# Gate and up as seven block products for eight, four token parts for three, and a down projection of its own

## The chip, the cores and the metric

The kernel runs on one core of one Trainium2 chip. Its time is the device time of one execution in microseconds; the figure of a kernel is the median of its runs. Three runs of the kernel before gave 2277.26, 2278.34 and 2279.22 us. A profile is one further execution, recorded instruction by instruction.

## The reference, cut to what matters

One decoder layer for a prompt of 1024 tokens and 8 single-token samples, so 1032 token columns. A wide input projection feeds a gated delta rule (8 heads) and a sliding-window attention; both are projected back, gated and mixed. What the change is about follows that:

```
h  = rmsnorm(x, norm1_w) * (1 + sc1) + sh1
z  = h @ w_in                       # q|k|v, gates, beta, decay, attention, two branch gates
...
mix = (sigmoid(ga) * y_a + sigmoid(gb) * y_b) @ w_o
x   = x + gt1 * mix
h2  = rmsnorm(x, norm2_w) * (1 + sc2) + sh2
gate, up = h2 @ w_ffn_gate, h2 @ w_ffn_up            # 1024 -> 2816 each
gc  = causal_dwconv(gate_ext, ffn_conv_w, L) + ffn_conv_b    # three taps along the tokens
x   = x + gt2 * ((silu(gc) * up) @ w_ffn_down)       # 2816 -> 1024
y   = rmsnorm(x, final_norm_w)
```

D_MODEL is 1024 (8 blocks of 128), D_FF is 2816 (22 tiles of 128). Beside y, the states (delta matrices, conv rows, caches, the last gate rows) are outputs. All is float32.

## The kernel before, in words

Activations lie transposed: features on the 128 partitions, tokens along the free dimension. The 1032 tokens are cut in three parts (`PARTS`, 384, 384 and 264), because a matmul's result must fit one PSUM bank. Each float32 operand is split in two float32r numbers, hi and lo (`split`, L115: a copy on ScalarE, L117, and a subtraction on VectorE, L118), and every product is three matmuls (`mm3`, L157 to L161: hi x hi, hi x lo, lo x hi). A full tile of 128 output features is 8 blocks of k, three parts and three matmuls (`project_steps`, L140): 72 matmuls, with an evacuation function called after each part. Weights come by `load_w` (L128): one DMA on SyncE's queue, then the split.

The stages, in order:
- Start and attention (0 to about 425 us): modulation vectors, the first norm (`modulate_part`, L279, which splits h part by part into the pool b1), key, query and value tiles, softmax.
- Delta rule (to about 1165): for each head `delta_prepare`, `unit_inverse` and `delta_scan` (L828, eight chunks one after the other; L843, L846, L850 and L854 are its matmuls), with the projections for head h + 2 beside them. The streams are given to `weave` (L1121) with start priorities; a planner orders the instructions of all engines by a simulated timeline and these priorities, and that order is fixed in the program. The tiles of the two branch gates (`gates`, L1144) are a generator that yields after each k: `pieces` (L746) draws 8 steps at a time, three times a head at a priority of 10000 behind the rest (L1463), and 24 times more in the last head (L743). They run in the one bank of `pmf`, ScalarE takes the tanh from it (L1157), GpSimd scales it, and a DMA stores it.
- Branches (to about 1380): what `gates` has left runs first in a plain loop (L1172), then the attention's output projection with the samples' delta rule between (`sample_delta`), then the delta rule's output projection.
- Residual and second norm (to about 1530): `residual` loads and transposes x, adds the gated w_o tiles to it (`add_gated`, L1248) and sums squares; it does so for parts 0 and 1, then for part 2, and `second_norm` (L1261) makes h2 in b1 for each part after its sums.
- Feed-forward (to about 2266): `ffn_tile` (L1342) does one gate tile and one up tile. ScalarE copies the gate out of PSUM into z (L1353), VectorE runs the three taps and the silu (L1357 to L1368), then multiplies by the up tile (L1377), and the result is split. Every two tiles, `ffn_down` (L1383) multiplies the pair before by its 128-row blocks of w_down and adds the product to x1 in SBUF, so down lies between gate and up tiles all along.
- The last norm (`last_norm`, L1400) runs part by part in the last down group.

The engine queues are in order, so an instruction that waits holds up what is behind it on its engine.

Of the kernel before, what the change touches and what calls it, by code (L numbers as in the profile page):

```python
# [28 lines left out]
PARTS = [(0, 384), (384, 384), (768, 264)]  # L29
# [28 lines left out]
class Step:  # L58
    def __init__(self, ctx, tc, I, O):
        self.ctx, self.tc, self.nc, self.I, self.O = ctx, tc, tc.nc, I, O  # L60
        self.cp = self.pool("cp", 1)
        self.dr = self.pool("dr", 1, DRAM)
        self.b1 = self.pool("b1", 1)
        self.wctx = ExitStack()
        self.where = self.pool("wp", 1, ctx=self.wctx), 2, 1
        self.pmm = self.pool("pmm", 2, PSUM)
        self.pmf = self.pool("pmf", 1, PSUM)
        self.mm, self.turn = [self.pmm], 0
        self.n, self.bufs = 0, {}
        self.lo_engine = None  # L70
        self.filler, self.ahead = iter(()), False

    def pool(self, name, bufs, space=None, ctx=None):
        kw = {} if space is None else {"space": space}
        if space != DRAM:
            kw["reuse_waits"] = "tile"
        return (ctx or self.ctx).enter_context(self.tc.tile_pool(name=name, bufs=bufs, **kw))
# [7 lines left out]
    def const(self, shape, name, dt=F32):  # L85
        return self.cp.tile(shape, dt, tag=name, name=name)
# [33 lines left out]
    def load_split(self, pool, shape, src, tag, bufs, raws, rtag="raw"):  # L120

        raw = self.t(pool, shape, rtag, bufs=raws)
# [5 lines left out]
    def load_w(self, src, width=P, where=None):  # L128

        pool, bufs, raws = where or self.where  # L130
        return self.load_split(pool, [P, KC, width], src.rearrange("(k p) c -> p k c", p=P), "w", bufs, raws)
# [8 lines left out]
    def project_steps(self, w, X, evac, parts=(0, 1, 2), psum=None):  # L140
# [16 lines left out]
    def mm3(self, ps, whi, wlo, xhi, xlo, first, last):  # L157
        mm = self.nc.tensor.matmul
        mm(ps, whi, xhi, start=first, stop=False)  # L159
        mm(ps, whi, xlo, start=False, stop=False)  # L160
        mm(ps, wlo, xhi, start=False, stop=last)  # L161

    def new_parts(self):
        return [(self.t(self.b1, [P, KC, n], f"b1h{t}", F32R), self.t(self.b1, [P, KC, n], f"b1l{t}", F32R))
# [7 lines left out]
    def vectors(self, pool, psum):  # L172
# [24 lines left out]
        nc.vector.tensor_copy(self.fcw, ps[:, 256:344].rearrange("p (j n) -> p j n", j=4))  # L197
# [72 lines left out]
    def norm_part(self, pool, t, tags):  # L270

        lo, n = PARTS[t]
# [6 lines left out]
    def modulate_part(self, pool, psum, t, xs, a, sh):  # L279

        nc = self.nc
        hi, lo = self.h[t]
        n = PARTS[t][1]
        np_ = n // P * P
        shift = self.mT[:, sh:sh + 8, :]
        if n % P:
# [6 lines left out]
            self.split(hi[:, :, np_:n], lo[:, :, np_:n], v)  # L293
        for k in range(KC):
# [8 lines left out]
            self.split(hi[:, k, :np_], lo[:, k, :np_], v)  # L303
# [93 lines left out]
    def attention(self, pool, psum):  # L397
# [19 lines left out]
        for t in range(3):  # L417
# [51 lines left out]
    def key_pair(self, pool, i, kx):  # L469
# [5 lines left out]
        def k_out(t, ps):  # L475
# [10 lines left out]
            if t == 2:  # L486
                nc.vector.tensor_copy(kx[:, i, :], ps[:, P:P + 136])  # L487
# [8 lines left out]
    def query_pair(self, pool, qt):  # L496
# [4 lines left out]
        def q_out(t, ps):  # L501
# [8 lines left out]
            if t == 2:  # L510
                nc.vector.tensor_scalar_mul(self.qs[:, qt, :], ps[:, 256:264], 0.125)
# [491 lines left out]
    def sample_delta(self):  # L1003
# [3 lines left out]
        a, b, c, d, e = (self.t(self.b1, [P, KC, PARTS[t][1]], f"b1{x}{t}", F32R).bitcast(F32).rearrange("p k n -> p (k n)")  # L1007
                         for x, t in (("h", 1), ("l", 1), ("h", 2), ("l", 2), ("h", 0)))
        small = carver(d, e)
        S0 = []  # L1010
        for h in range(H):
            S0.append((a, b, c)[h // 3][:, h % 3 * NP:h % 3 * NP + NP].rearrange("p (b v) -> p b v", b=NS))
# [68 lines left out]
        for h in range(H):  # L1081
            if h % 4 == 0:
                yield
            db = self.t(self.b1, [P, KC, 384], "b1l0", F32R).bitcast(F32).rearrange("p k n -> p (k n)") if h == 0 else db
            d = db[:, h % 3 * NP:h % 3 * NP + NP].rearrange("p (b v) -> p b v", b=NS)
# [58 lines left out]
    def gates(self):  # L1144
# [6 lines left out]
        for i, (col, dst) in enumerate(tiles):  # L1151
            w, ahead = ahead or load(i), None

            def out(t, ps):
                lo, n = PARTS[t]
                s = self.t(self.gt[0], [P, 384], self.gt[1], bufs={"gt": 2, "sgx": 3}.get(self.gt[1]))[:, :n]
# [4 lines left out]
            for t in range(3):  # L1161
                for step in self.project_steps(w, self.h, out, (t,), self.pmf):
# [4 lines left out]
    def branches(self, pool, pool2):  # L1167
        nc, I = self.nc, self.I
        ub = [self.t(pool, [P, KC, n], f"t{t}", bufs=1) for t, (_, n) in enumerate(PARTS)]
        ob = [self.load_part(pool2, self.ob, t) for t in range(3)]  # L1170
        self.fill_where, self.gt, self.ahead = self.where, (pool, "sgx"), True
# [24 lines left out]
        for t in range(3):  # L1196
# [5 lines left out]
        for t in range(3):  # L1202
# [5 lines left out]
    def gate_part(self, pool, src, t):  # L1208
        s = self.t(pool, [P, 384], "sgx", bufs=3)[:, :PARTS[t][1]]
# [4 lines left out]
    def residual(self, xpool, pool, psum):  # L1214
        nc, I = self.nc, self.I
        self.x1 = [self.t(xpool, [P, KC, n], f"x1_{t}", bufs=1) for t, (_, n) in enumerate(PARTS)]
        for t, (lo, n) in enumerate(PARTS):
            for c in range(0, n, P):
                w = min(P, n - c)
                x = self.t(pool, [P, NT], "flo", bufs=3)  # L1220
                src = I["x_prompt"][0][lo + c:lo + c + P, :] if w == P else I["x_sample"].rearrange("b s d -> (b s) d")
                nc.sync.dma_start(x[:w, :NP], src)
                for k0 in (0, 4):
                    ps = self.t(psum, [P, 4, P], "xt", bufs=2)
                    for k in range(4):
                        self.transpose(ps[:, k, :w], x[:w, (k0 + k) * P:(k0 + k + 1) * P])
                    nc.scalar.copy(self.x1[t][:, k0:k0 + 4, c:c + w], ps[:, :, :w])
        self.h2 = {}
        for parts in ((0, 1), (2,)):
            sums, last = {}, {}  # L1230

            def add(t, ps):
                self.add_gated(t, ps, j, 16)
                sq = self.t(pool, [P, 384], "nsq", bufs=2)[:, :PARTS[t][1]] if j else                     self.t(pool, [P, 384], "nss", bufs=2)[:, :PARTS[t][1]]
                nc.scalar.activation(sq, self.x1[t][:, j, :], AF.Square)
                if j == 0:
                    sums[t] = sq
                elif j < 7:
                    nc.gpsimd.tensor_tensor(sums[t], sums[t], sq, op=ALU.add)
                else:  # L1240
                    last[t] = sq

            for j in range(8):
                self.project(self.load_w(I["w_o"][0][:, j * P:(j + 1) * P]), self.mix, add, parts=parts)
            for t in parts:
                self.h2[t] = self.second_norm(pool, psum, (sums[t], last[t]), t)

    def add_gated(self, t, ps, j, m):  # L1248

        nc = self.nc  # L1250
        n = PARTS[t][1]
        np_ = n // P * P
        x = self.x1[t][:, j, :]
        nc.vector.scalar_tensor_tensor(x[:, :np_], ps[:, :np_], self.mT[:, m + j, 8:9], x[:, :np_],  # L1254
                                       op0=ALU.mult, op1=ALU.add)
        if n % P:
# [4 lines left out]
    def second_norm(self, pool, psum, squares, t):  # L1261

        nc = self.nc
        x1, a2, sh = self.x1[t], self.a2, self.mT[:, 24:32, :]
        n = PARTS[t][1]
        np_ = n // P * P
        nc_ = (n + P - 1) // P
        rs = self.t(pool, [P, 4], "rs", bufs=2)
        nc.vector.memset(rs, 1.0)
        ss = self.t(psum, [P, 4], "ss", bufs=2)  # L1270
        r = self.t(psum, [P, 512], "ss", bufs=2)
        for c in range(nc_):
            w = min(P, n - c * P)
            for i, sq in enumerate(squares):
# [246 lines left out]
```

## Time and profile before

| | us |
|---|---|
| median of 3 runs | 2278.34 |
| profiled execution | 2281.89 |
| its span, first to last instruction | 2279.8 |
| PE busy | 2175.5 (95%) |
| VectorE busy | 1258.7 (55%) |
| ScalarE busy | 732.2 (32%) |
| GpSimd busy | 221.2 (10%) |
| DMA, mean over the span | 84 GB/s |
| mean granted TensorE clock | 0.965 |

PE is TensorE's matmuls, PEld its weight loads, DVE VectorE, ACT ScalarE, POOL GpSimd, SP SyncE, which issues most DMAs. A busy time is an average over stages with different limits. A row of the groups reads: line, engine, operation, output<-inputs, shape, count | busy us, mean ns of one | idle time of the engine just before, and what ended it. Matmuls overlap in the pipeline, so the mean duration of one is not the time that one more would add; for that the distance of their starts is read from the order of time. A row of a table by stretches gives the stretch, its length, the busy time and count of each engine, the granted clock, the share of the DMA engines and GB/s.

### The profile page before, as it was taken

The numbers are of one execution on the slowest core, as the hardware profiler recorded it, in microseconds if no ns is written. First come the engines' busy times: TensorE is split into PE (matmuls) and PEld (weight loads), VectorE is DVE, ScalarE is ACT, GpSimd is POOL, SyncE is SP. The second block draws the span as 40 slices with busy tenths as digits, with TensorE's granted clock in tenths as the row PEclk, the third lists the DMA queues.
The fourth block names the chain that finished last, engine by engine and source line by source line (L and its number), as shares of the span: only waits on it lengthen the run. The fifth ranks groups of instructions, "written<-read, shape, count | busy, mean of one in ns | idle before, by whom it ended". The sixth has DMA issues, their size and how long they took to land.

```text
span 2279.8 us, 37918 instructions
## 1 busy us (share of the span) xinstructions
PE 2175.5 (95%) x15311; PEld 2043.4 (90%) x15311; DVE 1258.7 (55%) x2714; ACT 732.2 (32%) x1838; POOL 221.2 (10%) x331
## 2 busy tenths in 40 slices
PE   7998999898999999999879999999999999999998
PEld 3795888698999999999768998989999999999997
DVE  4556666665366465474232752374555555555657
ACT  3445444433333434423320223352111222111112
POOL 2000000122212112112101100210000000000000
PEclk8999998899999999999979999989999999999999
DMA  9312322322222222222432834222101111111111
GB/s 335 130 39 82 114 78 94 102 63 70 75 61 80 66 60 75 67 64 72 128 123 87 271 93 138 85 66 65 46 29 47 56 56 47 47 33 42 56 49 75
DMA packets 272768, 191.96 MB, mean 84 GB/s; under 512 B 54286, under 2 KB 248881, under 8 KB 272578
## 3 DMA queue, kind: packets, MB, share of 16 engines
q1 hardware_dynamic: 272594, 189.55, 27.4%
q8 instruction: 120, 1.97, 0.4%
q14 instruction: 54, 0.44, 0.1%
HBM read 159.62 MB, written 32.27 MB: 84 GB/s over the span
## 4 chain that ended last, share of the span: by engine, by line
PE 86%; DVE 4%; DMA 4%; ACT 2%; issue 1%; SPq 1%; POOL 0%; DVEq 0%; POOLq 0%; ACTq 0%
PE mm L159 24%; PE mm L161 24%; PE mm L160 24%; PE pv L591 1%; PE pv L589 1%; DMA qst<-in_w_mod_dram 1%; PE mm L243 1%; PE pt L169 1%; PE tp L169 1%; PE rc L850 1%; PE rc L846 1%; PE sc L552 1%; PE mm L1052 1%; PE tp L809 1%; PE tp L808 1%
## 5 line engine op out<-in xcount | busy, mean ns | idle before, releaser
L159 PE MATMUL mm<-b1h,wh 128*128 128x384 f32 (+1 forms) x2688 | 877.5, 327 | 13.7 <-DVE kx L487 4.5
L161 PE MATMUL mm<-b1h,wl 128*128 128x384 f32 (+1 forms) x2688 | 869.9, 324 | 4.0 <-DVE wl L118 4.0
L160 PE MATMUL mm<-b1l,wh 128*128 128x384 f32 (+1 forms) x2688 | 869.9, 324 | 0.3 <-DVE b1l L118 0.2
L159 PEld LDWEIGHTS mm<-b1h,wh 128*128 128x128 f32 x2688 | 511.0, 190 | 28.2 <-issue 6.3
L160 PEld LDWEIGHTS mm<-b1l,wh 128*128 128x128 f32 x2688 | 511.1, 190 | 9.6 <-issue 6.4
L161 PEld LDWEIGHTS mm<-b1h,wl 128*128 128x128 f32 x2688 | 510.4, 190 | 7.1 <-DVE wl L118 4.9
L118 DVE TENSOR_TENSOR wl<-raw,wh 128x1024 fp32r<-128x1024 f32 x136 | 166.4, 1224 | 244.6 <-ACT wh L117 243.4
L117 ACT ACTIVATE wh<-raw 128x1024 fp32r<-128x1024 f32 x137 | 144.3, 1053 | 280.1 <-PE mm L160 252.2
L1254 DVE SCALAR_TENSOR_TENSOR x<-mm,mT,x 128x384 f32<-128x384 f32 (+1 forms) x288 | 163.4, 572 | 112.2 <-PE mm L161 103.5
L159 PE MATMUL mm<-fhi,wdh 128*128 128x384 f32 (+1 forms) x528 | 170.8, 324 | 1.0 <-ACT wdh L117 0.7
L161 PE MATMUL mm<-fhi,wdl 128*128 128x384 f32 (+1 forms) x528 | 168.2, 320 | 0.3 <-DVE wdl L118 0.3
L160 PE MATMUL mm<-flo,wdh 128*128 128x384 f32 (+1 forms) x528 | 168.3, 319 | 0.0
L159 PE MATMUL mm<-b2h,wh 128*128 128x384 f32 (+1 forms) x384 | 124.4, 325 | 6.6 <-ACT b2h L117 6.6
L161 PE MATMUL mm<-b2h,wl 128*128 128x384 f32 (+1 forms) x384 | 123.4, 322 | 1.0 <-DVE wl L118 1.0
L160 PE MATMUL mm<-b2l,wh 128*128 128x384 f32 (+1 forms) x384 | 124.0, 323 | 0.3 <-DVE b2l L118 0.3
L117 ACT ACTIVATE fhi<-fa 128x384 fp32r<-128x384 f32 (+1 forms) x66 | 29.5, 485 | 223.9 <-PE mm L161 192.3
L159 PEld LDWEIGHTS mm<-fhi,wdh 128*128 128x128 f32 x528 | 99.1, 188 | 2.4 <-ACT wdh L117 1.2
L161 PEld LDWEIGHTS mm<-fhi,wdl 128*128 128x128 f32 x528 | 98.9, 188 | 1.0 <-DVE wdl L118 1.0
L160 PEld LDWEIGHTS mm<-flo,wdh 128*128 128x128 f32 x528 | 99.2, 188 | 0.0
L159 PEld LDWEIGHTS mm<-b2h,wh 128*128 128x128 f32 x384 | 73.6, 192 | 7.8 <-ACT b2h L117 7.0
L1363 POOL COPY fzl<-fz 128x10 f32<-128x10 f32 x22 | 20.8, 947 | 600.0 <-ACT fz L1353 600.0
L161 PEld LDWEIGHTS mm<-b2h,wl 128*128 128x128 f32 x384 | 73.3, 191 | 1.7 <-DVE wl L118 1.7
(439 smaller groups left out, 2937.7 us busy)
## 6 DMA issues: line engine op xcount, KB each, us to landing
raw<-in_w_in_dram SPq DMA_DIRECT2D x60, 512.0 KB
raw<-in_w_ffn_gate_dram SPq DMA_DIRECT2D x22, 512.0 KB
raw<-in_w_ffn_up_dram SPq DMA_DIRECT2D x22, 512.0 KB
raw<-in_w_ffn_down_dram SPq DMA_DIRECT2D x22, 512.0 KB
qst<-in_w_mod_dram SPq DMA_DIRECT2D x16, 512.0 KB
raw<-in_w_mod_dram SPq DMA_DIRECT2D x16, 512.0 KB
raw<-in_w_o_dram SPq DMA_DIRECT2D x16, 512.0 KB
wmh<-in_w_mod_dram SPq DMA_DIRECT2D x8, 512.0 KB
```

What stands on the lines that cost most here:

```text
L117: self.nc.scalar.activation(hi, x, AF.Copy)
L118: (eng or self.nc.vector).tensor_tensor(lo, x, hi.bitcast(F32), op=ALU.subtract)
L159: mm(ps, whi, xhi, start=first, stop=False)
L160: mm(ps, whi, xlo, start=False, stop=False)
L161: mm(ps, wlo, xhi, start=False, stop=last)
L169: self.nc.tensor.transpose(out, in_, self.ident[:p, :p])
L243: nc.tensor.matmul(ps[32 * j:32 * j + 32], self.cT[:, k0 + j, :], ws[j // 2][:, j % 2, :], start=k0 == 0, stop=k0 > 0)
L552: nc.tensor.matmul(sc[:, r, 256 - w:256], q, KH[:, lo:lo + w], start=True, stop=False)
L589: nc.tensor.matmul(out, V[:, n, ch], pc[:, r::2, :], start=True, stop=n == 0)
L591: nc.tensor.matmul(out, V[:, n - 1, ch], pp[:, r::2, :], start=False, stop=True)
L808: nc.tensor.matmul(kk[:, 0, c, :], K[:, c0 + c, :], K[:, c0 + c, :], start=True, stop=True)
L1254: nc.vector.scalar_tensor_tensor(x[:, :np_], ps[:, :np_], self.mT[:, m + j, 8:9], x[:, :np_], op0=ALU.mult, op1=ALU.add)
```

## The change

**Parts.** The tokens are cut in four parts of 256, 256, 260 and 260 everywhere. Row loads of x keep the old cut (`ROWS`), so a piece of h out of one row block goes to two parts. `gates` is drawn by the same `pieces` as before.

**Gate and up.** Parts are taken in two pairs ("halves"). For a pair of token parts, the four k blocks below and above 512, and two tiles of output features, the 2 x 2 block product is done by seven products for eight. `second_norm` makes, for each half, seven split operands (two blocks and five sums and differences) in place of h2. `pair_weights` makes seven split weights out of a 1024 x 256 block, with four sums on GpSimd. `pair_product` runs the seven products; some go on adding to a bank whose value was copied out first (`keep`), and VectorE adds kept values at evacuation. The factor 0.5 of the silu is moved into the conv weights.

**Order.** Activations go to DRAM as they are done, x1 too (`output_pass`, after the w_o tiles), and down is a stage behind all of gate and up: it reloads x1 and the activations, splits weights and activations for four tiles at a time, and adds a product over four tiles to x1.

Cut to its core:

```diff
-PARTS = [(0, 384), (384, 384), (768, 264)]
+PARTS = [(0, 256), (256, 256), (512, 260), (772, 260)]
+HALF = [(0, 512), (512, 520)]
+ROWS = [(0, 384), (384, 384), (768, 264)]
...
 def modulate_part(self, pool, psum, t, xs, a, sh):
...
-            self.split(hi[:, k, :np_], lo[:, k, :np_], v)
+            for q, (lo, m) in enumerate(PARTS):
+                c, e = max(lo, r0), min(lo + m, r0 + np_)
+                if c < e:
+                    self.split(*(a[:, k, c - lo:e - lo] for a in self.h[q]), v[:, c - r0:e - r0])
...
 def gates(self):
...
-            for t in range(3):
-                for step in self.project_steps(w, self.h, out, (t,), self.pmf):
+            for t in range(4):
+                for step in self.project_steps(w, self.h, out, (t,), self.fill_psum):
...
+    def output_pass(self, pool, p, where):
...
+        for j in range(8):
+            self.project(self.load_w(I["w_o"][0][:, j * P:(j + 1) * P], where=where), self.mix, add, parts=(2 * p, 2 * p + 1))
+            nc.sync.dma_start(self.x1d[j][:, c:c + n], self.x1[p][:, j, :])
+            yield
...
+    def second_norm(self, pool, psum, p):
...
+        a1, a2, b1, b2 = (x1[:, k:k + 4, c:c + n] for c in (0, n) for k in (0, 4))
...
+        self.split(*ops[0], a1)
+        self.split(*ops[1], a2)
+        minus(v, a1, b1, a1)
+        minus(v, d, b2, a1)
+        minus(g, b1, b2, b1)
+        minus(g, a2, a2, d)
+        for op, x in zip(ops[2:], (d, a1, b1, a2, b2)):
+            self.split(*op, x)
+            yield
...
+    def pair_weights(self, pool, w, f):
...
+        def calc(x, y, op):
+            s = self.t(pool, [P, 4, P], "ws", bufs=4)
+            self.nc.gpsimd.tensor_tensor(s, x, y, op=op)
+            return s
...
+        out = [put(a0), put(b0)]
+        s1 = calc(a1, b1, ALU.add)
+        s2 = calc(s1, a0, ALU.subtract)
+        out += [put(s2), put(s1)]
+        s3 = calc(a0, a1, ALU.subtract)
+        s4 = calc(b0, s2, ALU.subtract)
+        return out + [put(s3), put(b1), put(s4)]
+
+    def pair_product(self, pool, psum, w, pairs, evac):
...
+            for k in range(4):
+                self.mm3(ps, wh[:, k, :], wl[:, k, :], xh[:, k, :], xl[:, k, :], first and k == 0, k == 3, **kw)
...
+        for p in pairs:
+            x[p] = bank(self.pmm, "mm", width[p])
+            product(x[p], p, 0)
+            keep(p, 0)
+        for p in pairs:
+            y[p] = bank(psum, "wy", width[p])
+            product(y[p], p, 1)
+            evac(p, 0, 0, y[p], r[p, 0])
+        for p in pairs:
+            product(x[p], p, 2, False)
+            keep(p, 1)
+        for p in pairs:
+            v[p] = bank(psum, "wv", width[p])
+            product(v[p], p, 3)
+        for p in pairs:
+            product(x[p], p, 4, False)
+            keep(p, 2)
+            evac(p, 1, 1, v[p], r[p, 2])
+        for p in pairs:
+            product(x[p], p, 5, False)
+            evac(p, 1, 0, x[p], None)
+        for p in pairs:
+            product(v[p], p, 6, False)
+            evac(p, 0, 1, v[p], r[p, 1])
+
+    def ffn_gate_up(self, pool, pool2, psum, f, w, first):
...
+        for pairs in ((0,), (1,)) if first else ((0, 1),):
+            self.pair_product(pool, psum, w, pairs, gate)
+        w = self.pair_weights(pool, I["w_ffn_up"][0], f)
...
+        self.pair_product(pool, psum, w, (0, 1), up)
...
+    def ffn_down(self, pool, psum):
+        group, turn = 4, 6
...
+                raw = self.t(self.pw, [P, NP], "raw", bufs=3)
+                nc.sync.dma_start(raw, I["w_ffn_down"][0][f * P:(f + 1) * P, :])
...
+                nc.sync.dma_start(raw, self.act[f])
+                acts.append(room(1, f, NT))
+                self.split(*acts[-1], raw)
+                if f == 1:
+                    for j in range(8):
+                        for p, (c, n) in enumerate(HALF):
+                            nc.scalar.dma_start(self.x1[p][:, j], self.x1d[j][:, c:c + n])
...
+                self.weave((self.output_pass(pool, 0, where), 0, 1))
+                self.weave((self.output_pass(pool, 1, where), 0, 1), (self.second_norm(pool, psum, 0), 30, 22))
...
+                    w = self.pair_weights(pool, self.I["w_ffn_gate"][0], 0)
+                    self.weave((self.second_norm(xr, psum, 1), 0, 1))
```

446 lines of the change are left out of this document (264 added, 182 removed).

## The prediction, made before the change was run

> **What bounds the kernel now.** I read the page from the top: busy times, then the chain that ended last, then the table by stages, the groups of instructions, and last the order of time.
>
> ```profile
> span 2279.8 us, 37918 instructions
> ...
> PE 2175.5 (95%) x15311; PEld 2043.4 (90%) x15311; DVE 1258.7 (55%) x2714; ACT 732.2 (32%) x1838; POOL 221.2 (10%) x331
> ...
> PE 86%; DVE 4%; DMA 4%; ACT 2%; issue 1%; SPq 1%; POOL 0%; DVEq 0%; POOLq 0%; ACTq 0%
> PE mm L159 24%; PE mm L161 24%; PE mm L160 24%; PE pv L591 1%; PE pv L589 1%; DMA qst<-in_w_mod_dram 1%; PE mm L243 1%; PE pt L169 1%; PE tp L169 1%; PE rc L850 1%; PE rc L846 1%; PE sc L552 1%; PE mm L1052 1%; PE tp L809 1%; PE tp L808 1%
> ```
>
> TensorE holds 86% of the chain that ended last, and 72% is the three lines of `mm3`. By stages (attention; delta rule; branches; residual with second norm; feed-forward; last rows; columns: stretch, length, then busy time and count of PE, PEld, DVE, ACT, POOL, then granted clock):
>
> ```profile
> 0.00:425.00 425.00, 386.04 (x2315) 299.86 (x2316) 255.96 (x688) 202.91 (x630) 19.70 (x55) 0.93 0.35 118
> 425.00:1165.00 740.00, 706.13 (x6128) 677.23 (x6127) 401.51 (x872) 264.52 (x780) 131.70 (x192) 0.97 0.28 75
> 1165.00:1380.00 215.00, 202.34 (x1297) 197.94 (x1298) 110.74 (x214) 45.11 (x63) 16.82 (x10) 0.96 0.49 152
> 1380.00:1530.00 150.00, 140.78 (x864) 133.23 (x863) 71.32 (x152) 66.19 (x116) 25.27 (x23) 0.92 0.34 100
> 1530.00:2266.00 736.00, 734.65 (x4688) 731.79 (x4687) 410.45 (x763) 149.38 (x239) 25.49 (x47) 1.00 0.16 49
> 2266.00:2280.00 14.00, 5.59 (x27) 3.39 (x25) 8.75 (x26) 4.12 (x13) 2.25 (x5) 0.62 0.39 154
> ```
>
> The feed-forward stretch is TensorE without a hole, at full clock: matmuls taken out there come off the time one for one. The delta stage is denser than its work needs, because the 16 gate tiles are fed into its holes. So two things decide: what one narrow matmul costs, and where the gate tiles go.
>
> **Counts.** `mm3` ran on three sets of operands, of which two are shown (b1, and the activations before down):
>
> ```profile
> L159 PE MATMUL mm<-b1h,wh 128*128 128x384 f32 (+1 forms) x2688 | 877.5, 327 | 13.7 <-DVE kx L487 4.5
> ...
> L159 PE MATMUL mm<-fhi,wdh 128*128 128x384 f32 (+1 forms) x528 | 170.8, 324 | 1.0 <-ACT wdh L117 0.7
> ```
>
> A full tile is 8 k x 3 parts x 3 = 72 matmuls, so b1 is 3 x 2688 / 72 = 112 tiles (60 of w_in, 8 of w_o, 44 of gate and up); the two output projections of `branches`, on b2, are 8 each. Gate and up are 44 x 72 = 3168 matmuls, down 3 x 528 = 1584, w_o 576, the other 76 tiles 5472: 10,800. After: gate and up 11 pairs x 2 matrices x 2 halves x 7 products x 12 = 3696; down 22 x 8 x 4 x 3 = 2112; w_o 768; the 76 tiles 7296: 13,872. One eighth of the products goes, but every tile of the kernel is cut in four parts for three.
>
> **Price of one.** Durations overlap, so I count starts: 24 matmuls of 264 columns from the first row to the second, 48 of 384 from there to the third.
>
> ```profile
> 1698.84 0.28 PE L159 MATMUL mm<-b1h,wh 128*128 128x264 f32 x1
> ...
> 1701.77 0.34 PE L159 MATMUL mm<-b1h,wh 128*128 128x384 f32 x1
> ...
> 1710.25 0.28 PE L159 MATMUL mm<-b1h,wh 128*128 128x264 f32 x1
> ```
>
> 2.93 us / 24 = 122.1 ns and 8.48 us / 48 = 176.7 ns; mean of the old widths 158.5 ns. Slope 0.455 ns a column, 2 ns fixed: 118.5 ns at 256, 120.3 at 260, mean 119.4. Lower bound: pure width, 118.7. Upper bound: 122 ns is itself a floor, then every narrow matmul costs 122.1. I take 119.4, since 122.1/176.7 is 0.69 as 264/384 is. By it:
> - gate and up 3168 x 158.5 = 502.1 us to 3696 x 119.4 = 441.3: -60.8
> - down 251.1 to 252.2: +1.1; w_o 91.3 to 91.7: +0.4
> - the 76 tiles ahead 867.3 to 871.1: +3.8
> Together -55.5 us.
>
> **Gate tiles.** `pieces` takes 48 lots of 8 steps, one part each: 24 in eight heads, 24 more in the last. Three parts a tile made 48, all of it. Four make 64, so 16 parts (4 tiles, 16 x 24 x 119.4 ns = 45.8 us) fall to the loop in `branches`, where nothing needs filling. Rows: all 48 on record; L846, the scan, in heads 6 and 7; four rows from the end of the scan.
>
> ```profile
> L1157 ACT ACTIVATE gt<-mm x48: 372/491/493, 475.6 to 1126.1; 128x384 f32<-128x384 f32 x32, 128x264 f32<-128x264 f32 x16
> ```
> ```profile
> 1039.00:1106.00 67.00, 3.28 (x16) 2.58 (x16) 1.00 0.24 65
> 1117.00:1157.00 40.00, 5.24 (x16) 3.48 (x16) 0.70 0.50 131
> ```
> ```profile
> 1144.13 0.79 PE L846 MATMUL rc<-y,W 128*128 128x128 f32 x2 [0.25 <-DVE y L844]
> ...
> 1147.85 0.80 PE L846 MATMUL rc<-y,W 128*128 128x128 f32 x2
> ...
> 1161.85 1.11 PE L169 MATMUL rc<-ident,vn 128*128 128x128 f32 x4 [3.94 <-DVE vn L872]
> 1169.60 0.69 PE L159 MATMUL mm<-b2h,wh 128*128 128x384 f32 x1 [6.64 <-ACT b2h L117]
> ```
>
> Alone a chunk of the scan takes 3.72 us, 30 for eight; woven with filler it took 67, nearly alone 40. So with less filler the last two heads draw together; head 7's inverse has its own chain before its scan, so I allow 20 us of a possible 27. And the moved parts need only h and weights, so they fill the hole from about 1157.9 to 1169.6, 11 us beside four transposes. Of 45.8, 15 are left: **+15** (0 if all is absorbed, 45.8 if nothing).
>
> **Gate and up around the matmuls.** A pair of tiles is 336 matmuls, 40.1 us.
>
> ```profile
> L118 DVE TENSOR_TENSOR wl<-raw,wh 128x1024 fp32r<-128x1024 f32 x136 | 166.4, 1224 | 244.6 <-ACT wh L117 243.4
> L1359 DVE SCALAR_TENSOR_TENSOR fa<-fz,fcw,fa 128x1024 f32<-128x1024 f32 x40 | 51.4, 1285 | 1.0 <-DVE fa L1364 0.3
> L118 DVE TENSOR_TENSOR flo<-fa,fhi 128x384 fp32r<-128x384 f32 x44 | 23.4, 554 | 2.7 <-ACT fhi L117 1.4
> L1377 DVE SCALAR_TENSOR_TENSOR fa<-mm,fa 128x264 f32<-128x264 f32 x22 | 9.5, 430 | 21.4 <-PE mm L161 21.4
> ```
> ```profile
> L1353 ACT COPY fz<-mm 128x264 f32<-128x264 f32 x22 | 8.0, 363 | 2.4 <-PE mm L161 2.4
> ```
>
> From 554 and 1224 ns, 512 columns cost DVE 0.69 us, a conv step 0.75. Per pair DVE has 14 weight splits (9.6), 20 evacuations of 256 (0.42 each, 8.4) and four convs (about 2.8 each, 11): 29 of 40.1 us. ACT adds 12 copies of kept products at 0.36. The shortest distance is product 5 back on the bank of product 4: one product, 1.43 us, against a 0.36 us copy that may stand behind one more ACT instruction. Eight weight sums go to POOL, and POOL and DVE get in each other's way; smallest, median and longest of one DVE instruction beside POOL's:
>
> ```profile
> L1089 DVE SCALAR_TENSOR_TENSOR b1h<-b1h,egb,b1l x40: 334/340/2510, 1246.5 to 1281.8; 128x128 f32<-128x128 f32 x40
> ```
> ```profile
> 1248.86 1.90 POOL L1087 TENSOR_TENSOR b1l<-b1l,kq 128x1024 f32<-128x1024 f32 x1
> ```
>
> A POOL sum of 512 would be about 1 us, so up to 8 us a pair block DVE: 37 of 40.1 at worst. The Trainium skill, "SBUF — State Buffer", section "SBUF: two separate sides", says that the shared port pair is an exclusive lock between a GpSimd instruction and a VectorE one with two SBUF inputs; by it the splits and convs here queue whole behind POOL, and the 340 to 2510 ns agree. By the rule DVE is 92% full, by its busy time alone 72%; the sum would differ by the bank waits. I take **+9** for the stage (0 to +43; the top is DVE at 44 us a pair).
>
> **The seams and the rest.** The old seam between second norm and gate:
>
> ```profile
> 1497.00:1518.00 21.00, 17.29 (x58) 12.66 (x59) 15.03 (x45) 13.60 (x29) 0.96 (x2) 0.60 0.09 26
> ```
>
> DVE 15 and ACT 14 of 21 us bounded it. Now the second half's norm is 520 columns for 264, with seven operand splits of 1.24 us and differences, some 24 us on DVE, under 10 us of first-half gate products plus 10 us in which products and splits go in step; weight splits wait in the same queue. **+6** (-5 to +15). Seam to down: the first four tiles' rooms come free with products 0 to 3 of the last up, 8.6 us before its end; act raws come two at a time, and x1 must be back for the first `add_gated`, behind seven banks of 1.4 us. The x1 loads stand in ACT's queue, and splits behind them. **+4** (0 to +12). `modulate_part` splits in 48 pieces for 24, each extra piece 0.15 us, the fixed part of the two L118 rows above: **+3** (0 to +7). Stores of act and x1, some 31 MB with their loads, double 49 GB/s in a stretch whose neighbours ran at 152: 0; a load late by a few us would show at a seam, and is in those bounds. SP issues the stores; prefetch behind them is 20 us ahead: 0. The last group stays: 0.
>
> **Sum.** -55.5 + 15 + 9 + 6 + 4 + 3 = -18.5 us. The profiled execution took 2281.9 us around its span of 2279.8, so 2263.4; the median of the runs is 3.6 lower: **2260 us**.
>
> **Rivals.**
> - The gate tiles cost nothing: all 45.8 hide. For: the scan's 3.72 against 8 us; against: the inverse's own chain. -33.5: 2245.
> - Slower: the gate tiles are not absorbed. The delta stage keeps its 740 us as a chain of waits, and 45.8 us are added whole: -18.5 + 30.8 = +12.3, 2291. It decides where less than 12.3 us of 45.8 is absorbed. For: filler runs at lowest priority and still started at 475, so the plan has holes from the start; against: the 67 against 40 us.
> - Gate and up bound by DVE: 44 us a pair, 11 x 3.9 - 9 = +34 more: 2294. For: 92% with POOL; against: slack of 1.4 to 4.3 us at every bank.
> - A floor per matmul: 122.1 at any width, 13,872 x 2.7 ns = +37: 2297. Against it are 128-wide loads and matmuls at 0.45 us for four, 111 ns:
>
> ```profile
> 442.70 0.38 PE L808 MATMUL tp<-K 128*128 128x128 f32 x2
> ...
> 443.15 0.39 PE L808 MATMUL tp<-K 128*128 128x128 f32 x2
> ```
>
> The Trainium skill, "TensorE: Matmul & The Clock Gate", section "Back-to-back issue gap", gives 81 ns sustained at 128 columns and 131 at 512, a fixed 64 ns; by it 109 ns before and 98 after, an estimated +180 us. The rows disagree: 177 and 122 where it has 114 and 99.
>
> **Chances and range.** Forecast 0.57, gate tiles free 0.14, not absorbed 0.12, DVE 0.12, floor 0.05. About 0.2%, 4.6 us, is what a measurement tells from no change. The forecast's own range is 2240 to 2276, nearly all faster; the three slow rivals lose some of their time to good luck in another term, and 0.07 of their 0.29 falls within 0.2%. Faster 0.70, same 0.08, slower 0.22. The range reaches to the free gates with a lucky seam, 2228, and to the DVE rival, 2294.
>
> **What would show it.** Starts of 256-column matmuls 118 to 119 ns apart; the gate-and-up stretch near 450 us, the down stretch near 256, both with PE at its length; `gt` 48 times and `sgx` written by 16 tanh after 1150; the delta stage ending 15 to 25 us earlier, the branches 30 longer. The forecast is wrong if the starts are 122 apart, if the delta stage ends where it did, or if PE idles on DVE in the pair products.

## The result, and the profile after

The changed kernel takes 2287.79 us (median of 5 runs, 2285.76 to 2292.12), the kernel before in the same comparison 2279.22 (2277.26 to 2281.30). The ratio is 1.0040, with a 95% interval of 1.0025 to 1.0055: slower by 9 us, where 19 us less were forecast. The profiled execution took 2289.57 us around a span of 2287.6, 7.7 us over the profiled one of before.

The page of the changed kernel, its span, busy times, and the chain that ended last by engine:

```profile
span 2287.6 us, 45274 instructions
...
PE 2146.6 (94%) x18405; PEld 2029.4 (89%) x18405; DVE 1359.8 (59%) x2947; ACT 823.5 (36%) x2132; POOL 376.4 (16%) x446
...
PE 78%; DVE 7%; DMA 5%; issue 3%; ACT 2%; POOL 1%; SPq 1%; ACTq 0%; DVEq 0%; POOLq 0%
```

PE is busy for 29 us less and the execution is 8 us longer. The chain shows the gap: TensorE held 86% of it before and 78% now, VectorE 4% and now 7%.

Where the time went is read from the same stages in both traces. The stretches are: delta rule to its last transposes, branches to their last product, residual to the last w_o product, and the feed-forward to its last down product. Columns as in the prediction: stretch, length, busy time and count of PE, PEld, DVE, ACT and POOL, granted clock, DMA share, GB/s. Before:

```profile
425.00:1163.00 738.00, 706.13 (x6128) 677.23 (x6127) 400.76 (x872) 264.52 (x780) 131.70 (x192) 0.97 0.28 75
1163.00:1380.40 217.40, 202.74 (x1299) 198.14 (x1299) 111.49 (x215) 45.11 (x63) 16.82 (x10) 0.95 0.49 151
1380.40:1492.50 112.10, 107.04 (x701) 104.79 (x701) 43.92 (x84) 42.34 (x69) 23.28 (x20) 0.97 0.42 125
1492.50:2266.30 773.80, 768.29 (x4848) 760.13 (x4846) 438.16 (x836) 173.22 (x286) 27.57 (x51) 0.99 0.16 48
```

After, with the feed-forward cut in gate and up (to 2009) and down:

```profile
425.00:1130.00 705.00, 678.90 (x6897) 656.16 (x6898) 397.34 (x870) 261.94 (x809) 131.05 (x194) 0.97 0.25 67
1130.00:1412.50 282.50, 250.07 (x1998) 245.19 (x1997) 127.48 (x264) 57.37 (x97) 25.27 (x24) 0.94 0.51 149
1412.50:1538.00 125.50, 112.15 (x886) 108.16 (x885) 61.04 (x99) 52.18 (x89) 36.26 (x28) 0.93 0.46 143
1538.00:2009.00 471.00, 456.47 (x3756) 454.16 (x3756) 356.16 (x610) 198.72 (x387) 159.38 (x136) 0.97 0.26 84
2009.00:2272.50 263.50, 258.27 (x2158) 256.93 (x2157) 146.48 (x342) 40.11 (x53) 2.22 (x4) 0.99 0.27 93
```

| stage | before | after | change | forecast |
|---|---|---|---|---|
| delta rule | 738.0 | 705.0 | -33.0 | -15 to -25 |
| branches | 217.4 | 282.5 | +65.1 | some +30 |
| together, all ahead of w_o | 1380.4 | 1412.5 | +32.1 | +21.8 (3.8 + 15 + 3) |
| residual, w_o | 112.1 | 125.5 | +13.4 | +0.4 |
| gate, up and down | 773.8 | 734.5 | -39.3 | -40.7 |
| last rows | 13.5 | 15.1 | +1.6 | 0 |
| span | 2279.8 | 2287.6 | +7.8 | -18.5 |

The feed-forward did what was forecast. The loss lies ahead of it: 10 us more than allowed up to the end of the branches, 13 us in the stage that had been costed at nothing.

**The price again.** Two 384-column matmuls of the branches before, 26 starts apart:

```profile
1338.99 0.33 PE L159 MATMUL mm<-b2h,wh 128*128 128x384 f32 x1
...
1343.50 0.33 PE L161 MATMUL mm<-b2h,wl 128*128 128x384 f32 x1
```

After, 260 columns in the branches, 24 starts apart, and seven products of gate and up (48 matmuls of 256 columns, 36 of 260):

```profile
1349.05 0.29 PE L167 MATMUL mm<-b2h,wh 128*128 128x260 f32 x1
...
1351.92 0.28 PE L167 MATMUL mm<-b2h,wh 128*128 128x260 f32 x1
```

```profile
1700.78 0.29 PE L167 MATMUL wy<-pk,sb 128*128 128x256 f32 x1
...
1710.76 0.28 PE L167 MATMUL wy<-b1l,sb 128*128 128x260 f32 x1
```

The new widths are as forecast: 2.87 us / 24 = 119.6 ns, 9.98 us / 84 = 118.8 ns. But in the branches a 384-column matmul took 4.51 us / 26 = 173.5 ns, not the 176.7 that the prediction read from 48 starts in the feed-forward and used everywhere. Those 48 are high for their own stage too: over the whole feed-forward the mean is 175.0 (means here and below are of neighbours of one width, without distances more than 15% off the median). At 173.5 and 121 ns the 76 tiles ahead cost 3648 x 173.5 + 1824 x 121 = 853.6 us before, and 7296 x 119.2 = 869.7 after: +16 where +3.8 stood in the sum. With each stage's own means (174.5 in the attention, 173.9 in the delta rule, 173.5 in the branches; after, 118.6 to 119.6) it is +12, so I give it as 12 to 16.

**The gate tiles.** Evacuations of gate parts, first those in the delta stage, then those left for the branches:

```profile
L1169 ACT ACTIVATE gt<-mm x48: 366/384/392, 475.2 to 1109.2; 128x256 f32<-128x256 f32 x24, 128x260 f32<-128x260 f32 x24
```
```profile
L1169 ACT ACTIVATE sgx<-mm x16: 367/385/399, 1126.5 to 1180.9; 128x256 f32<-128x256 f32 x8, 128x260 f32<-128x260 f32 x8
```

48 and 16, as forecast. The delta stage gave back 33 us for them.

**PE's waits in the branches** (what it waited for, us in total, times, longest), 1130 to 1412:

```profile
PE mm L167 <- DVE t L1191: 19.2, 4, 9.9
PE mm L167 <- ACT sgx L1169: 8.3, 1, 8.3
```

The 8.3 us are a queue: three banks hold finished gate parts, and their tanh stands in ScalarE's queue behind 16 splits that wait for loads of the attention's output. Such a hole costs more than its length: behind it, from 1148.4 to 1153.8, the granted clock was 0.50, and the next 260-column matmuls started 217 ns apart, for 120 again from 1154 on. The 19.2 us are evacuations of output-projection tiles that wait for gate rows or for VectorE, which is then in `sample_delta`, whose states are loaded into the buffers of h: at 1172 to 1187, for 1118 to 1133 before, because the left-over gate tiles still read h (read from the program; no run moved it alone).

**The start of the w_o tiles.** The last product of the branches and the first w_o product, before and after, and SyncE's queue after:

```profile
1380.13 0.28 PE L161 MATMUL mm<-b2h,wl 128*128 128x264 f32 x1
...
1390.30 0.69 PE L159 MATMUL mm<-b1h,wh 128*128 128x384 f32 x1 [0.38 <-ACT wh L117]
```
```profile
1412.18 0.28 PE L169 MATMUL mm<-b2h,wl 128*128 128x260 f32 x1
...
1433.62 0.58 PE L167 MATMUL mm<-b1h,wh 128*128 128x256 f32 x1 [4.24 <-ACT wh L125]
```
```profile
1415.31 1.42 SPq L1354 DMA_DIRECT2D raw<-in_state_ffn_conv_dram  x3
...
1428.40 9.96 SPq L131 DMA_DIRECT2D raw<-in_w_o_dram  x5
```

The first w_o product comes 21.4 us after the last product of the branches, for 10.2 before, with 94 transposes between (72 of x, 22 of the rows of `ffn_states`) for 24. So 11 of the 13 us are lost ahead of the first w_o product; from it to the last one the trace has 104.3 us for 102.1.

The rows of `ffn_states` (L1354) take all three `raw` buffers, which had a tag of their own before. They come free with transposes that stand behind all transposes of x, so the first w_o weights are asked for at 1428.

**The second norm.** Second half, in order of time:

```profile
1566.14 7.93 POOL L1329 TENSOR_TENSOR x<-x 128x1040 f32<-128x1040 f32 x1 [1.33 <-ACT b1h L125]
...
1574.10 1.07 ACT L125 ACTIVATE b1h<-x 128x1040 fp32r<-128x1040 f32 x1 [5.24 <-POOL x L1329]
...
1575.49 0.58 PE L167 MATMUL mm<-pk,sb 128*128 128x256 f32 x1 [2.02 <-ACT r L1412]
```

One GpSimd subtraction takes 7.93 us; the next one of the same size took 2.39 (at 1574.03). ScalarE waits 5.24 us for it with a split, and behind that split stands the copy (L1412) that frees the next bank. VectorE runs six instructions without a pause in the 5.7 us from 1566.1, and GpSimd's ends 2.3 us behind the last of them. The 40 us of this seam:

```profile
1540.00:1580.00 40.00, 26.09 (x143) 24.01 (x142) 32.67 (x40) 21.89 (x38) 23.71 (x15) 0.67 0.14 46
```

VectorE is busy for 32.7 of them, GpSimd for 23.7, PE for 26.1 at a clock of 0.67.

### The profile page after: what moved, and what is told of

It is laid out like the page before. It is cut to its first block, busy times and chain, and to the rows that moved or that the text cites. A ratio compares the mean times of both kernels' runs of the same rounds, so it can differ in the third digit from the quotient of the medians.

```text
span 2287.6 us, 45274 instructions
## 1 busy us (share of the span) xinstructions
PE 2146.6 (94%) x18405; PEld 2029.4 (89%) x18405; DVE 1359.8 (59%) x2947; ACT 823.5 (36%) x2132; POOL 376.4 (16%) x446
## 4 chain that ended last, share of the span: by engine, by line
PE 78%; DVE 7%; DMA 5%; issue 3%; ACT 2%; POOL 1%; SPq 1%; ACTq 0%; DVEq 0%; POOLq 0%
PE mm L167 17%; PE mm L169 17%; PE mm L168 17%; PE wv L169 3%; PE wv L167 3%; PE wv L168 3%; PE wy L167 2%; PE wy L169 2%; PE wy L168 2%; PE pv L602 1%; PE pv L600 1%; PE tp L177 1%; PE pt L177 1%; PE sc L563 1%; PE rc L857 1%
## 5 line engine op out<-in xcount | busy, mean ns | idle before, releaser
L167 PE MATMUL mm<-b1h,wh 128*128 128x256 f32 (+1 forms) x2176 | 635.8, 293 | 31.6 <-ACT sgx L1169 8.3
L169 PE MATMUL mm<-b1h,wl 128*128 128x256 f32 (+1 forms) x2176 | 627.1, 289 | 3.2 <-DVE wl L126 3.2
L168 PE MATMUL mm<-b1l,wh 128*128 128x256 f32 (+1 forms) x2176 | 626.0, 288 | 0.0
L169 PEld LDWEIGHTS mm<-b1h,wl 128*128 128x128 f32 x2176 | 418.3, 193 | 7.8 <-DVE wl L126 5.0
L167 PE MATMUL mm<-b2h,wh 128*128 128x260 f32 (+1 forms) x512 | 147.9, 290 | 23.0 <-DVE t L1191 19.2
L169 PE MATMUL mm<-b2h,wl 128*128 128x260 f32 (+1 forms) x512 | 146.0, 287 | 1.1 <-DVE wl L126 1.1
L168 PE MATMUL mm<-b2l,wh 128*128 128x260 f32 (+1 forms) x512 | 146.3, 286 | 0.0
L167 PE MATMUL mm<-pk,sb 128*128 128x256 f32 x352 | 100.4, 285 | 5.0 <-ACT r L1412 5.0
L169 PE MATMUL mm<-pk,sb 128*128 128x256 f32 x352 | 100.4, 285 | 0.1
L168 PE MATMUL mm<-pk,sb 128*128 128x256 f32 x352 | 99.6, 283 | 0.0
L168 PEld LDWEIGHTS mm<-b2l,wh 128*128 128x128 f32 x512 | 99.0, 193 | 0.0
L1412 ACT COPY r<-mm 128x256 f32<-128x256 f32 (+1 forms) x132 | 49.2, 374 | 100.4 <-PE mm L169 85.8
L169 PE MATMUL mm<-b1h,sb 128*128 128x260 f32 x264 | 75.4, 286 | 0.0
L167 PE MATMUL mm<-b1h,sb 128*128 128x260 f32 x264 | 75.3, 285 | 0.0
```

What stands on the lines that cost most here:

```text
L167: mm(ps, whi, xhi, start=first, stop=False, **kw)
L168: mm(ps, whi, xlo, start=False, stop=False, **kw)
L169: mm(ps, wlo, xhi, start=False, stop=last, **kw)
L1412: nc.scalar.copy(r[p, i], x[p])
```

## The experiments

Each was compared with the kernel before in runs on the same chip; the medians of before in the groups were 2284.9, 2283.6 and 2282.8, so ratios are compared, and 0.001 is 2.3 us. Where I speak of stalls, it is the sum over all matmuls of a stage of the distance to the next start beyond the pitch of its width.

### Are the left-over gate tiles the loss?

First theory: delta stage and branches lost 31 us together because 16 parts were moved; so put them back.

```diff
-                yield from self.pieces(3)
+                yield from self.pieces(4)
...
-                               (self.pieces(3), 10000, 100)]
+                               (self.pieces(4), 10000, 100)]
```

> The changed kernel, with its gate tiles drawn four lots at a time for three (32 in the eight heads, 32 more in the last), so that all 64 parts run inside the delta stage as they did before the change. Theory (the 16 gate parts left over for the branches cost the loss): against the kernel before, the change's delta stage ends 34 us earlier and its branches take 65 us longer, 31 us in all; with the parts back the delta stage takes about 738 us again and the branches about 220, and the whole is 25 to 31 us shorter than the changed kernel, 2257 to 2263 us. Rival (the narrow parts themselves, with more evacuations, cost it in both places): the branches shrink by the 46 us of matmuls and the delta stage grows by nearly as much, no more than 8 us is gained, 2280 or above.

Ratio 0.9987 (0.9974 to 0.9999), some 11 us under the changed kernel: neither theory's number (the rival's 2280 or above holds, its gain of no more than 8 does not). Its evacuations show why:

```profile
L1169 ACT ACTIVATE gt<-mm x64: 365/383/390, 480.2 to 1191.1; 128x256 f32<-128x256 f32 x32, 128x260 f32<-128x260 f32 x32
```

All 64 were drawn there, and eight were still evacuated after the last transposes of the scan, at 1149 (none of 48 in the kernel before, whose scan ended at 1163). By 970 us the kernel before had evacuated 34 of its parts and this one 30, though it draws four for three: I read this as the plan putting about one part into a hole, whatever its width, so that a narrower part fills less of it. Drawing more of them does not undo the move.

The same two steps on the kernel before, with four parts and no other part of the change:

```diff
-PARTS = [(0, 384), (384, 384), (768, 264)]
+PARTS = [(0, 256), (256, 256), (512, 256), (768, 264)]
+ROWS = [(0, 384), (384, 384), (768, 264)]
```

> The kernel before with one thing of the change alone: four token parts (256, 256, 256, 264) for three, the gate tiles drawn as they were, three lots at a time; gate, up and down are done as before. Theory (gate tiles left over): 16 gate parts fall to the branches here too, so it loses the 31 us that delta stage and branches lost together in the change, and little else, as a narrow matmul costs 118 to 122 ns for 177: 2308 to 2316 us. Rival (the loss comes from the new feed-forward and its seams, and narrow parts cost nothing ahead of it): 2279 to 2287.

> The kernel before with four token parts and the gate tiles drawn four lots at a time, so that all of them run inside the delta stage. Theory (gate tiles left over): nearly nothing is lost against the kernel before, 2279 to 2287 us (the matmuls grow by some 10 us in all at 119.4 ns each). Rival (the narrow parts cost it wherever they are): as the kernel with four parts and three lots, 2300 or above.

1.0254 (1.0236 to 1.0273) and 1.0247 (1.0226 to 1.0269): 58 and 56 us lost, more than any theory had, and equal. Stages of the second (delta rule, branches, residual, feed-forward without its end), and PE's first wait in its feed-forward from 1514 to 2200:

```profile
423.00:1134.60 711.60, 685.28 (x6991) 663.04 (x6989) 399.00 (x872) 264.72 (x813) 135.36 (x198) 0.99 0.26 68
1134.60:1401.30 266.70, 237.83 (x1876) 232.31 (x1875) 126.28 (x262) 52.37 (x91) 24.37 (x20) 0.94 0.50 146
1401.30:1513.90 112.60, 107.76 (x890) 105.63 (x891) 46.92 (x101) 45.87 (x86) 23.84 (x27) 0.97 0.42 124
1513.90:2320.00 806.10, 780.66 (x6435) 769.44 (x6433) 455.45 (x974) 181.68 (x338) 27.23 (x51) 0.99 0.16 46
```
```profile
PE mm L160 <- DVE fa L1382: 14.9, 16, 1.6
```

The branches end at 1401, 21 us later than before. The sum of the pitches there is 16 us larger and the stalls 5 us, so with most gate parts inside the delta stage the width alone costs what the price again said. The first of the two, with 16 parts left over as in the changed kernel, starts the last matmul of its branches at 1403.4, the second at 1401.0, and the changed kernel at 1412.2. So with the same parts left over the old program loses 9 us less in front: about half of what the changed kernel loses there beyond the pitch hangs on something else that it does. The 19.2 us of waits at output-projection tiles are absent here. The old feed-forward loses 33 us more (2334 - 1514 = 820 us for 787): PE now waits for VectorE at the narrow parts, 14.9 us, and by the pitch 66 tiles of 96 narrow matmuls for 72 are some 14 us longer (an estimate, at 0.2 us a tile). The wait does not carry over to the changed kernel, whose product stage has no such wait. So these two showed the width in front, and confounded the total with a stage that the change had replaced.

### The front in its old parts

Second theory: the front lost it twice, by pitch and by left-over parts. The changed kernel with three parts up to the end of the branches; the mixed result is cut to the four parts as it is split, and the samples' states lie in the old layout of h again.

```diff
+PARTS = [(0, 384), (384, 384), (768, 264)]
+BACK = [(0, 256), (256, 256), (512, 260), (772, 260)]
...
-            self.split(self.mix[t][0][:, j, :], self.mix[t][1][:, j, :], u)
+            for q, (lo, m) in enumerate(BACK):
+                c, e = max(lo, r0), min(lo + m, r0 + n)
+                if c < e:
+                    self.split(*(x[:, j, c - lo:e - lo] for x in self.mix[q]), u[:, c - r0:e - r0])
```

The changed kernel itself stood beside it:

> The changed kernel itself, unchanged, so that the kernels of this round stand beside it on the same chip. As in its first runs: 1.0025 to 1.0055 of the kernel before.

> The changed kernel with the old three token parts (384, 384, 264) from the start to the end of the branches, and its four parts from the w_o tiles on. Theory (the front lost it: 76 tiles at 173.4 and 121.1 ns in the three widths take 853 us, in four widths at 119.2 ns 869 us, and 16 gate parts left over make holes in the branches): the branches end at 1380 to 1385 us as in the kernel before, for 1412, and the time is 27 to 32 us below the changed kernel, 0.989 to 0.993 of the kernel before. Rival (the front is a chain of waits and the filler runs in its holes, so that width and left-over parts matter little, and the loss is at the entry to the residual stage and in the seams): less than 10 us below the changed kernel.

The changed kernel: 1.0035 (1.0019 to 1.0050). With the old front: 0.9904 (0.9885 to 0.9923), 2263.3 us, 30 us less and in the theory's range. Its delta rule, branches and residual:

```profile
425.00:1167.00 742.00, 708.72 (x6136) 678.40 (x6136) 402.33 (x873) 265.31 (x782) 129.61 (x193) 0.97 0.28 75
1167.00:1384.30 217.30, 202.94 (x1302) 198.23 (x1302) 113.78 (x238) 47.10 (x86) 17.39 (x10) 0.95 0.51 154
1384.30:1513.60 129.30, 114.92 (x889) 111.15 (x887) 61.25 (x100) 52.34 (x90) 36.37 (x28) 0.91 0.45 139
```

The branches take 217 us as in the kernel before. The residual stage keeps its 129 us, so its loss is not the front's.

That still leaves pitch, left-over parts and the buffers of h together. The next one has left-over parts at the old width:

```diff
-                yield from self.pieces(3)
+                yield from self.pieces(2)
...
-                               (self.pieces(3), 10000, 100)]
+                               (self.pieces(2), 10000, 100)]
```

> The changed kernel with the old three token parts to the end of the branches, and the gate tiles drawn two lots at a time for three, so that 16 of the 48 gate parts (16 x 24 matmuls of some 157 ns, 60 us) are left over for the branches, as 16 of 64 were in the changed kernel. Theory (left-over parts cost time by themselves, apart from the width): 8 to 18 us longer than with the three parts alone. Rival (the delta stage gets shorter by what leaves it, and only the narrow matmuls lost time in front): within 4 us of the three parts alone, 0.989 to 0.992 of the kernel before.

1.0042 (1.0023 to 1.0061): 31 us more than with the three parts alone, beyond both ranges (27 us between the two profiled executions). Its delta rule and branches:

```profile
425.00:1131.00 706.00, 669.34 (x5814) 638.90 (x5814) 393.02 (x861) 253.81 (x760) 118.08 (x178) 0.95 0.25 65
1131.00:1410.00 279.00, 256.42 (x1615) 251.84 (x1615) 123.08 (x249) 57.58 (x105) 27.77 (x24) 0.95 0.52 156
```

The delta rule got 36 us shorter and the branches 62 us longer, for 59 us of moved matmuls (10 of the parts are 384 wide, 6 are 264). The sum of the pitches is the same within 2 us; the stalls grew by 25 us, most of them in the branches, where PE waited 7.3 us for output-projection tiles and 3.9 for a tanh that stood behind the loads. So in this layout left-over parts cost time at an unchanged width: 16 wide ones cost 31 us, where the changed kernel with 16 narrow ones has 16 to 20 us of stalls in front (32.1 less the pitch). That they cost what they fail to fill is my reading; the kernel before with four parts and 16 of them left over lost 9 us less in front than the changed kernel.

### The entry to the residual stage

```diff
                     self.residual(pool, psum)
-                    self.ffn_states(pool, psum)
...
                     self.weave((self.output_pass(pool, 0, where), 0, 1))
+                    self.ffn_states(pool, psum)
```

> The changed kernel with ffn_states called after the first output pass for before it. Theory (the first w_o weights are loaded late because the three raw buffers are held by the conv-state rows, whose transposes stand behind those of x): the first w_o product comes 8 to 12 us earlier, and the w_o tiles end 8 to 12 us sooner after the branches (126 us now). Rival (x's own loads and transposes set the start of the w_o tiles): no more than 3 us.

1.0023 (1.0009 to 1.0037) against 1.0035: 3 us, which the intervals do not separate. Beside the trace of the unchanged kernel in the same group, the first w_o product comes 13.8 us after the last product of the branches, for 24.4: 10.6 us earlier, as the theory had it. But from the first to the last w_o product it is 110.8 us for 104.6, so the stage takes 124.6 us for 129.0.

```profile
1427.79 0.39 PE L167 MATMUL mm<-b1h,wh 128*128 128x256 f32 x1 [1.10 <-ACT wh L125]
```

The late weights are there, and the stage gains less than half of what the first product gains: 56 of the 72 transposes of x still stand ahead of it (24 before), and what no longer stands there runs between the products.

### GpSimd and VectorE in the second norm

```diff
-        minus(g, b1, b2, b1)
-        minus(g, a2, a2, d)
+        minus(v, b1, b2, b1)
+        minus(v, a2, a2, d)
```

> The changed kernel with the two differences that second_norm gives to GpSimd (L1329 and L1330) on VectorE, twice, once for each half. Theory (VectorE and GpSimd block each other there): in the second half the difference took 7.93 us on GpSimd beside VectorE's work and TensorE had three holes of 8 us together around it; on VectorE it is a 1.2 us instruction, and the whole is 4 to 6 us shorter. Rival (VectorE's own work bounds the seam): 5 us more work on VectorE for the two halves, and the time is the same or up to 3 us longer.

1.0001 (0.9987 to 1.0015), 8 us under the changed kernel's 1.0035 and 1.0040; the intervals do not overlap. The differences of the form that took 7.93 us:

```profile
L1329 DVE TENSOR_TENSOR x<-x x4: 1208/1222/1776, 1517.7 to 1575.0; 128x1024 f32<-128x1024 f32 x2, 128x1040 f32<-128x1040 f32 x2
```

That row holds the two that moved and two that had been there; the longest is 1.78 us. More work on the engine that the rival called the bound, and less time, more than the 4 to 6 us of the theory: beside the trace of the unchanged kernel in the next group on the same chip, the w_o tiles gain 2 us and the feed-forward 4.5.

### Is VectorE the bound of gate and up?

```diff
         for p in pairs:
-            product(x[p], p, 5, False)
             evac(p, 1, 0, x[p], None)
```

> The changed kernel with the sixth of the seven products of each pair left out (an eighth of the gate and up tiles is then short of a term); splits, sums and evacuations are all kept. Theory (TensorE bounds gate and up, each matmul costs 118 to 120 ns): 528 matmuls by 119 ns are gone, 63 us. Rival (VectorE with GpSimd is nearly the bound, 37 of 40 us a pair at worst): with 34.3 us of matmuls a pair VectorE takes over, and less than 40 us are gained.

0.9901 (0.9881 to 0.9920), 30 us less: half of the matmul time that went. A stretch of 100 us of gate and up with six products, then with seven, and the longest waits with six (1600 to 1900):

```profile
1700.00:1800.00 100.00, 94.99 (x775) 93.77 (x774) 86.22 (x145) 38.33 (x84) 35.17 (x32) 0.98 0.27 87
```
```profile
1700.00:1800.00 100.00, 100.00 (x843) 100.00 (x842) 75.32 (x136) 41.12 (x83) 32.87 (x31) 1.00 0.23 75
```
```profile
POOL ws L1378 <- DVE sb L126: 115.4, 41, 8.1
ACT fz L1473 <- DVE fa L1466: 65.6, 25, 3.6
```

With seven products a pair takes 40 us of matmuls and PE has no idle time in the stretch. With six it has 34.3 us, and the rest of the work takes over at 34.3 + (62.8 - 33.0) / 11 = 37.0 us (the end of the kernel after w_o got 33.0 us shorter). The prediction had 37 us as VectorE's load when GpSimd blocks it; that the two figures agree, and that GpSimd and ScalarE wait for VectorE above all, fits the rival, though VectorE is busy for 86 of the 100 us and not all. The rival was wrong for this kernel by 3 us a pair, and 37 us a pair is what bounds the next saving.

### Together

> The changed kernel with three changes together: the old three token parts to the end of the branches, ffn_states after the first output pass, and second_norm's two GpSimd differences on VectorE. Theory (the three work in different places and add): 0.9904 of the kernel before with the three parts alone, less 2 to 5 us for the conv-state rows and 4 to 8 us for the differences: 0.985 to 0.988, 2250 to 2257 us. Rival (what the last two free is taken by the next wait in the seam): 0.990, as with the three parts alone.

```diff
-                    w = self.pair_weights(pool, self.I["w_ffn_gate"][0], 0)
+                    w = self.pair_weights(pool, self.I["w_ffn_gate"][0], 0, nc.vector)
```

> As front3_mend, and the four weight sums of the first gate pair (L1378), which GpSimd does in the seam between second norm and gate, on VectorE. Theory (VectorE waits for GpSimd there: two instructions on dg took 1.48 to 2.52 us together for 0.48): 2 to 5 us shorter than front3_mend, though VectorE gets four instructions of about 0.7 us more. Rival (VectorE's own work and the chain of the norm set the seam): the same or up to 3 us longer.

0.9872 (0.9854 to 0.9890), then 0.9847 (0.9829 to 0.9865): 2254.2 and 2248.5 us. The first theory held; the second gain, 5.7 us, lies just above its range. The intervals of the two overlap, but all four runs of the second are shorter than all four of the first. Of the 4.3 us between their spans, 1.2 lie ahead of the w_o tiles, where the two programs do the same. The longest instruction on dg, in the norm's chain, falls from 1308 to 760 ns; that this is what gained the time was not shown. The last version is 1.5% faster than the kernel before and 1.9% faster than the change.

## Why the prediction was wrong, point by point

- **Price of one, 119.4 ns: right** (118.8 to 119.6), as are all counts. The means of 256 and 260 columns lie below the 122.1 of the floor. The rule of the Trainium skill, "TensorE: Matmul & The Clock Gate", section "Back-to-back issue gap", by which an estimated 98 ns would stand, does not hold for these matmuls.
- **The 76 tiles, +3.8: the step that failed first.** The new price was right, the old one was read from 48 starts of another stage: 176.7 ns there, 175.0 over that whole stage, 173.5 to 174.5 in the stages ahead. Over 3648 wide matmuls that is 8 to 12 us, and the term is +12 to +16.
- **w_o, +0.4: the step that failed next.** Only the matmuls were counted (+1.7 by the pitch); the stage took 13.4 us more, 11 of them ahead of the first w_o product. Three things were not costed: the transposes of x, 72 of which now stand ahead of that product and 24 before; the tag `raw`, now shared by w_o weights and conv-state rows, so that the weights come late; and the first half's second norm, which now runs beside the second w_o pass, with GpSimd work in it. Moving the rows gave 4 us in the trace, the differences 2; no run put the transposes back between the products, so their share was not measured by itself.
- **Gate tiles, +15, and modulate_part, +3: right in size.** 32.1 less 12 to 16 of pitch leaves 16 to 20 for both. The parts fell out as forecast and the delta stage shrank by 33 us, more than the 20 allowed; the branches lost more than allowed, with PE waiting at the tanh queue and at tiles held up by late gate rows and by `sample_delta`. The size came out, but not as 15 us of matmuls left unhidden alone: the kernel before with four parts and 16 of them left over loses 9 us less in front. How the 16 to 20 split stays open. The rival of a delta stage that keeps its 740 us was wrong, though its 2291 lies near the result.
- **Gate and up, -60.8: right within 2 us.** 3696 x 118.8 = 439 us, for 498 at the feed-forward's means (175.0 and 121.4 ns).
- **Bank waits, +9: wrong, next to nothing.** PE has no hole in the steady stretch. The slack is 3 us a pair.
- **Seam second norm to gate, +6: within its bounds, near +7.** Stalls there are 21 us from 1540 to 1580, against 14 before from 1490 to 1520; two runs that took work from GpSimd gained 8 and 6 us, both partly ahead of the seam. The rule of the Trainium skill on the shared ports ("SBUF — State Buffer", section "SBUF: two separate sides") spoke against this part of the change. The trace agrees: the subtraction of 7.93 us, against 2.39, ended only after VectorE's six instructions.
- **Seam to down, +4: low.** One hole of 5 us at 2016 and a slower start behind it, some 7 us together. It is the risk that the prediction named, the reload of x1: PE waits for VectorE's first addition of a down product, and that waits for x1.

```profile
2020.89 0.48 DVE L1277 SCALAR_TENSOR_TENSOR x<-mm,mT,x 128x256 f32<-128x256 f32 x1 [4.54 <-DMA x<-x1d]
```

- **Tail, 0: +1.6.**

The sum misses by 26 us: 10 in front, where the price of the old width alone is 8 to 12, 13 in the stage costed at nothing, and 3 behind it. There too high a wait at the banks and too low a price of the seams nearly cancelled, which was luck.

## What to carry to other kernels

Take the price of a removed and of an added instruction from the stage in which it stands, and from many starts, not from 48: 2% on the price of what goes away, over thousands of instructions, was as large as half the gain that was forecast. A change of tile width is paid by everything that shares the tiling; keep the narrow tiles to the stage that needs them. Count a stage whose matmuls stay the same as changed when its buffers or its neighbours change.

## What the hardware showed that I had not expected

The same 384-column matmul starts every 173.5 ns in the branches and every 175.0 ns in the old feed-forward (means of 706 and 2963 distances); in the stretch of the feed-forward that the prediction read, the distances alternate between 174 and 179 or 180 ns, at a granted clock of 1.00. At 264 columns the means are 121.0 and 121.4 (367 and 1443 distances). What makes the difference was not found.

A GpSimd subtraction of 128x1024 or 128x1040 took from 2.4 to 7.9 us beside VectorE's instructions, and VectorE does the same in 1.2. Work given to GpSimd lengthened a seam in which VectorE was already busy for 33 of 40 us.
